# Mixture of experts with soft routing: the third product of the main phase split a second time

## The chip, the cores and the metric

The kernel runs on one core of one Trainium2 chip. The metric is device time in microseconds, the median of several runs. The engines are TensorE (PE in the profile; PEld is its weight load), VectorE (DVE), ScalarE (ACT), GpSimd (POOL) and SyncE (SP). Here POOL and SP mostly issue DMA transfers.

## The reference

Every token takes part in all eight experts, weighted by a softmax of its router logits.

```python
# x: 16 x 512 x 512, router_logits: 16 x 512 x 8, expert_weights: 8 x 512 x 2048, all float32
probs = exp(router_logits - max) / sum
for e in range(8):
    output += probs[:, :, e:e+1] * matmul(x, expert_weights[e])     # 16 x 512 x 2048
```

Written as one product, `output = Z W`. Z has 8192 rows (the tokens) and 8 x 512 columns (x times the probability of each expert), W has 8 x 512 rows and 2048 columns.

## The kernel before

**Two levels of Strassen's products.** The token rows are cut into pieces of 256 (HQ); piece 2q is a, piece 2q+1 is b. With the experts in two halves and the 2048 columns in two halves of 1024, each pair (a, b) is a 2 x 2 block product, done with seven products P1 to P7 in place of eight (Winograd's form). Each of these is itself a product of K = 4 experts x 512 with 1024 columns. Four of the seven (P1, P5, P2, P4) are split once more: the function `sub_product` takes two pieces of 256 rows at once, and does seven inner products in place of eight; `inner_weights` makes the seven weights from four blocks by three or four subtractions. P1, P5 and P2 are kept in DRAM (`kept`, one tensor for each pair), P4 goes to the output as a first part of one quarter.

**The main phase** does the three that are left, P6, P3 and P7, for all q from 0 to 15, one unit of 128 rows of a and 128 rows of b at a time (u = 0, 1), and in it for each half n of 512 columns. For each (q, u, n):

- three loads of kept results, m1, m5 and m2 (`from_kept`, on SP);
- ScalarE copies m1 into a PSUM bank x (L511), and P6's 16 matmuls add to it. The sum is called U2 in the change's title;
- C11 = m1 + m2 on VectorE, and out by POOL (`put`, L506);
- m1 = x + m5 on VectorE (U2 + P5), then P3's 16 matmuls into a bank of their own, and C12 = P3 + m1, out by POOL;
- P7's 16 matmuls into bank x; ScalarE copies it (L522), and POOL adds that to the output in DRAM, over P4 (an accumulating transfer, L523);
- C22 = x + m5 on VectorE, put off to the beginning of the next turn (`late`), out by POOL.

The left operands of the next unit are made on VectorE in seven steps (`operands`), spread over the turn: x times probabilities (z from xT and pT), and subtractions of two z tiles.

**Order.** A scheduler orders instructions and assigns buffers. In the main phase VectorE is kept in the order of the program (`pinned[0] = True` in `dve`); on the other engines the scheduler chooses. Each engine takes its instructions in order, and so do the two queues' issuers, SP and POOL: an instruction that waits holds those behind it. A tile whose buffer is to be used again waits until all that read the earlier tile are done, a transfer from it included.

**Buffers.** `wpool` has 12 tiles of 1 MB (weights), `zpool` 12 (left operands), `xpool` 8, and 21 `h` tiles of 128 x 512 float32 are handed out in turn (`h_tile`). There are eight PSUM banks.

**Lines in the profile.** Helpers issue most instructions: L103 is every tensor_tensor on VectorE (`tt`), L114 every plain transfer on SP (`sp`), L117 weight and x casts on POOL (`pool`), L123 every matmul (`mm`); L342 is `keep` in `sub_product`. So groups are told apart by their tiles.

Of the kernel before, what the change touches and what calls it, by code (L numbers as in the profile page):

```python
# [32 lines left out]
def kernel(  # L33
# [27 lines left out]
    out_f = out.flatten_outer_dims()  # L61

    dram = ctx.enter_context(tc.tile_pool(name="dram", bufs=1, space=bass.MemoryType.DRAM))
    wpool = ctx.enter_context(tc.tile_pool(name="wpool", bufs=12))
    zpool = ctx.enter_context(tc.tile_pool(name="zpool", bufs=12))
    xpool = ctx.enter_context(tc.tile_pool(name="xpool", bufs=8))
    spool = ctx.enter_context(tc.tile_pool(name="spool", bufs=5))
    hpool = ctx.enter_context(tc.tile_pool(name="hpool", bufs=1))
    cpool = ctx.enter_context(tc.tile_pool(name="cpool", bufs=1))

    with tc.tile_pool(name="psum0", bufs=1, space=bass.MemoryType.PSUM) as psum0:
        zero = spool.tile([P, NB], f16, name="zero", tag="xs")
        nc.vector.memset(zero, 0.0)
        every = psum0.tile([P, 8, NB], f32, name="every")
        for i in range(8):
            nc.tensor.matmul(every[:, i, :], zero[:, 0:P], zero, start=True, stop=True)
    psum = ctx.enter_context(tc.tile_pool(name="psum", bufs=8, space=bass.MemoryType.PSUM))

    K8 = 2 * C
    BLOCKS = ((0, 0), (1, 0), (0, 1), (1, 1))

    turn = count()

    def h_tile(shape, dtype):

        return hpool.tile(shape, dtype, name="h", tag=f"h{next(turn) % 21}")

    last = {}  # L90

# [10 lines left out]
    def tt(o, a, b, op):  # L102
        dve(nc.vector.tensor_tensor(out=o, in0=a, in1=b, op=op))  # L103
# [49 lines left out]
    def inner_weights(b, t3=None):  # L153
        t1 = new_w()
        tt(t1, b[0, 1], b[0, 0], SUB)
        yield
        t3 = t3 or b[0, 1]
        tt(t3, b[1, 1], b[0, 1], SUB)
        yield
        t2 = new_w()  # L160
        tt(t2, b[1, 1], t1, SUB)
        t4 = new_w()
        tt(t4, t2, b[1, 0], SUB)
        return {1: b[0, 0], 2: b[1, 0], 3: b[1, 1], 4: t4, 5: t1, 6: t2, 7: t3}


# [13 lines left out]
    P2, P1, PQ = 0, HE, 2 * HE  # L180


    def cast_x(row):
        xs = spool.tile([P, H], f16, name="xs", tag="xs")
        pool(xs, x_f[ds(row, P), :])
        return xs

    NF = 8
    early = [2 * HQ * (j // 2) + P * (j % 2) for j in range(NF)]
    lg0 = []  # L190
    for t in range(2):
        lg0.append(cpool.tile([P, 4, E], f32, name=f"lg0_{t}"))
        for j in range(0, 4, 2):
            sp(lg0[t][:, ds(j, 2)], lg_f[ds(early[4 * t + j], 2 * P), :].rearrange("(j p) e -> p j e", p=P))
    xs0 = [cast_x(row) for row in early[:2]]
    ident = cpool.tile([P, P], f16, name="ident")
    nc.vector.memset(ident, 1.0)
    nc.gpsimd.affine_select(out=ident, in_=ident, compare_op=mybir.AluOpType.is_equal, fill=0.0, base=0,
                            pattern=[[-1, P]], channel_multiplier=1)
    xs0 += [cast_x(row) for row in early[2:4]]  # L200
    b11 = {kn: new_w() for kn in BLOCKS}
    with behind():
        for kn in BLOCKS[:3]:
            for e in range(2):
                cast_w(11, kn, e, b11[kn])
    xs0 += [cast_x(row) for row in early[4:]]
    for e in range(2):
        cast_w(11, BLOCKS[3], e, b11[BLOCKS[3]])

# [51 lines left out]
    def load_x(h):  # L261
        xT = xpool.tile([P, C, HQ], f16, name="xT", tag="x")
        if h in x_dram:
            sp(xT, x_dram[h])
        else:
            for j in range(HQ // P):
                note(nc.sync.dma_start_transpose(out=xT[:, :, ds(j * P, P)], in_=cast_x(h * HQ + j * P)))
            x_new.append((h, xT))
        return xT

# [17 lines left out]

    kept = {r: [dram.tile([2, HQ, NB], f32, name=f"kept{r}_{i}") for i in range(NI)] for r in (1, 2, 5)}

    def half():
        return h_tile([P, NB], f32)

    def out_rows(i, odd, u, cols, n):
        return out_f[ds((2 * i + odd) * HQ + u * P, P), ds(cols * NH + n * NB, NB)]
# [4 lines left out]
        else:  # L300
            sp(kept[r][i][n, ds(u * P, P), :], t)

    def from_kept(r, i, u, n):
        t = half()
        sp(t, kept[r][i][n, ds(u * P, P), :])
        return t

    def sub_product(r, odd, first, w, prep, start=0, zs=None):

        for d in range(start, NI // 2):  # L310
# [19 lines left out]
            for u in range(HQ // P):  # L330
# [7 lines left out]
                    return banks[b]  # L338

                def keep(ps):  # L340
                    t = half()
                    nc.scalar.copy(t, ps)  # L342
                    return t

                def put(t, n, a, b, op):
                    o = half()
                    tt(o, a, b, op)
                    to_kept(r, 2 * d + t, u, n, o)

# [44 lines left out]
    def weights_of_t1():  # L394
        b = {}
        for i, kn in enumerate(BLOCKS):
# [4 lines left out]
        yield  # L401
        ready[5] = yield from inner_weights(b)
    pinned[0] = False
    sub_product(1, 0, P1, w, weights_of_t1(), 1,
                [[z.rearrange("p e c t -> p (e c) t") for z in zz] for zz in z1])

# [13 lines left out]
    def weights_of_t4():  # L420
        b = {}
        for i, kn in enumerate(BLOCKS):
            t, t2 = load(22, kn), load("t1", kn)
            if i < 3:
                b[kn] = load(21, kn)
            yield
            tt(t2, t, t2, SUB)
            store(22, kn, t)
            store("t2", kn, t2)
            if i == 3:  # L430
                b[kn] = load(21, kn)
                yield
            tt(b[kn], b[kn], t2, SUB)
        yield
        ready[4] = yield from inner_weights(b)
    sub_product(2, 0, P2, ready[2], weights_of_t4())


# [1 line left out]

    def weights_of_main():
        for kn in BLOCKS:
            t, t3 = load(22, kn), load(12, kn)
            yield
            tt(t3, t, t3, SUB)
            store("t3", kn, t3)
        yield
        for n in range(2):
            for w, what in ((w6, "t2"), (w3, 22), (w7, "t3")):
                for k in range(2):  # L450
                    w[k, n] = load(what, (k, n), False)
                if n == 0:
                    yield
    sub_product(4, 1, P2, ready[4], weights_of_main())

    def operands(xa, xb, pa, pb, t0):

        z = {}  # L460

        def step(r, x, p, e):
            z[r] = zpool.tile([P, HE, C, P], f16, name="z", tag="z").rearrange("p e c t -> p (e c) t")
            tt(z[r].rearrange("p (e c) t -> p e c t", e=HE),
               x[:, :, ds(t0, P)].unsqueeze(1).to_broadcast([P, HE, C, P]),
               p[:, :, ds(t0, P)].unsqueeze(2).to_broadcast([P, HE, C, P]), MUL)
        return z, [lambda: step(1, xa, pa[0], 0),
                   lambda: step(6, xb, pb[1], 0),
                   lambda: tt(z[6], z[6], z[1], SUB),
                   lambda: step(7, xb, pb[0], 0),  # L470
                   lambda: tt(z[7], z[1], z[7], SUB),
                   lambda: step(3, xa, pa[1], 0),
                   lambda: tt(z[3], z[3], z[6], SUB)]

    def units():
        for q in range(NI):
            xa, p1a = load_x(2 * q), load_p(2 * q, P1)
            xb, pqb = load_x(2 * q + 1), load_p(2 * q + 1, PQ)
            p1b, p2a = load_p(2 * q + 1, P1), load_p(2 * q, P2)
            for u in range(HQ // P):  # L480
                yield q, u, *operands(xa, xb, (p1a, p2a), (p1b, pqb), u * P)

    def prod(z, w, n, ps=None):
        start = ps is None
        if start:
            ps = bank()
        for k in range(2 * K8):
            mm(ps, z[:, k, :], w[k // K8, n][:, k % K8, :], start and k == 0, k == 2 * K8 - 1)
        return ps

    it = units()
    following = next(it)
    for step in following[3]:
        step()
    pinned[0] = True
    late = []
    while following:
        q, u, z, _ = following
        following = next(it, None)
        steps = following[3] if following else []  # L500
        for n in range(2):
            m1, m5, m2 = (from_kept(r, q, u, n) for r in (1, 5, 2))

            def put(odd, cols, o, a, b, op, q=q, u=u, n=n):
                tt(o, a, b, op)
                nc.gpsimd.dma_start(out=out_rows(q, odd, u, cols, n), in_=o)  # L506

            for args in late:
                put(*args)
            x = bank()  # L510
            nc.scalar.copy(x, m1)  # L511
            put(0, 0, m2, m1, m2, ADD)
            for step in steps[4 * n:4 * n + 2]:
                step()
            prod(z[6], w6, n, x)
            tt(m1, x, m5, ADD)
            for step in steps[4 * n + 2:4 * n + 4]:
                step()
            put(0, 1, m1, prod(z[3], w3, n), m1, ADD)
            prod(z[7], w7, n, x)  # L520
            c21 = half()
            nc.scalar.copy(c21, x)  # L522
            nc.gpsimd.dma_start(out=out_rows(q, 1, u, 0, n), in_=c21, accum_op=ADD)  # L523
            late = [(1, 1, m5, x, m5, ADD)]
            late = [(a, b, c, d, e, f, q, u, n) for a, b, c, d, e, f in late]
    for args in late:
        put(*args)

# [1 line left out]
_INS = ['x', 'router_logits', 'expert_weights']  # L530
_OUTS = [((16, 512, 2048), 'float32')]
# [25 lines left out]
```

## Time and profile before

| what | value |
|---|---|
| median of 3 runs | 1479.03 us (1478.55 to 1479.06) |
| the profiled execution's own time | 1482.83 us |
| its span, first to last instruction | 1481.1 us |
| mean granted TensorE clock | 0.992 |
| HBM read, written | 184.84 MB, 163.77 MB |
| matmuls ps<-w,z (L123) | 6672 |

A line of a group gives line, engine, operation, tiles, shapes and count, then total busy time and mean nanoseconds of one; behind the next bar stands the engine's idle time just before these instructions, with what ended most of it. "PE ps L123 <- DVE h L103: 11.8, 7, 3.0" in the view of waits says that matmuls of line 123 waited for VectorE's line 103, for 11.8 us in all, 7 times, at most 3.0. In a windows view each line is a stretch of time with the busy time (and count) of PE, PEld, DVE, ACT and POOL, the granted clock, the DMA engines' busy share, and GB/s. The mean of a matmul (380 ns) is longer than the distance from one to the next, since matmuls are pipelined; the same holds for VectorE and ScalarE by about 0.1 us. Landing is the time from a transfer's issue to its last semaphore update.

### The profile page before, as it was taken

Reading aid. Unit: us, or ns where it says so; the run is one execution under the profiler, and the core shown is the slowest. Engines: PE = TensorE matmul, PEld = TensorE weight load, DVE = VectorE, ACT = ScalarE, POOL = GpSimd, SP = SyncE. Lnnn points to the kernel's source line nnn. Section 1 sums busy time; section 2 is a strip of 40 time slices with the busy share of each in tenths; the row PEclk is TensorE's granted clock in tenths of the full one; section 3 lists DMA queues with packets and bytes.
Section 4 is the critical chain, followed back from the end, with each engine's and each line's share of the span. In section 5 each row is a group of like instructions: output and inputs, shape, how many; then the busy total and the mean of one; then the engine's idle time right before and its main releaser. Section 6 shows DMA issues by size and latency. Waiting matters only on the chain. (4 is left out here: it accounts for less than half of the span.)

```text
span 1481.1 us, 18273 instructions
## 1 busy us (share of the span) xinstructions
PE 1457.9 (98%) x6712; PEld 657.9 (44%) x6712; DVE 956.7 (65%) x1084; ACT 231.5 (16%) x414; POOL 243.4 (16%) x397
## 2 busy tenths in 40 slices
PE   7999999999999999999999999999999999999997
PEld 2444444444444444444444444444444444444443
DVE  4866676656586777766764566665666666565662
ACT  3211121111111121211111001011010101101010
POOL 3111100111000000010101222222222222222221
PEclk8999999999999999999999999999999999999999
DMA  9979967899749994379959887877777777777753
GB/s 174 198 187 259 266 166 182 199 264 255 210 152 305 362 333 148 114 225 258 320 191 319 275 229 212 234 209 219 212 213 210 205 233 207 227 220 214 214 142 91
DMA packets 195801, 327.83 MB, mean 221 GB/s; under 512 B 54784, under 2 KB 84480, under 8 KB 190080
## 3 DMA queue, kind: packets, MB, share of 16 engines
q1 hardware_dynamic: 136192, 203.97, 44.3%
q0 software_dynamic: 59520, 122.71, 35.4%
q8 instruction: 52, 0.85, 0.3%
q14 instruction: 37, 0.30, 0.1%
HBM read 184.84 MB, written 163.77 MB: 235 GB/s over the span
## 5 line engine op out<-in xcount | busy, mean ns | idle before, releaser
L123 PE MATMUL ps<-w,z 128*128 128x512 f16 x6672 | 1444.1, 380 | 3.0 <-DVE h L103 3.0
L123 PEld LDWEIGHTS <-z 128*128 128x128 f16 x6672 | 653.7, 98 | 793.2 <-issue 8.3
L103 DVE TENSOR_TENSOR h<-ps,h 128x512 f32<-128x512 f32 x378 | 260.4, 689 | 416.9 <-ACT h L522 213.2
L103 DVE TENSOR_TENSOR z<-xT,pT 128x2048 f16<-128x2048 f16 x248 | 297.1, 1220 | 19.4 <-PE ps L123 11.1
L103 DVE TENSOR_TENSOR z<-z 128x2048 f16<-128x2048 f16 x220 | 268.0, 1220 | 32.9 <-PE ps L123 24.9
L342 ACT COPY h<-ps 128x512 f32<-128x512 f32 x248 | 145.5, 587 | 601.6 <-PE ps L123 593.2
L506 POOL DMA_DIRECT2D out_dram<-h x192 | 115.3, 640 | 371.1 <-DVE h L103 353.3
L522 ACT COPY h<-ps 128x512 f32<-128x512 f32 x64 | 37.5, 586 | 600.8 <-issue 380.7
L117 POOL DMA_DIRECT2D xs<-in_x_dram x72 | 38.6, 539 | 312.4 <-DMA xT<-xs 304.3
L523 POOL DMA_DIRECT2D out_dram<-h x64 | 56.6, 885 | 177.0 <-ACT h L522 173.1
L103 DVE TENSOR_TENSOR w<-w 128x4096 f16<-128x4096 f16 x32 | 73.0, 2287 | 6.0 <-PE ps L123 3.1
L117 POOL DMA_DIRECT2D w<-in_expert_weights_dram x40 | 30.0, 766 | 131.9 <-DVE w L141 83.7
L103 DVE TENSOR_TENSOR h<-h,ps 128x512 f32<-128x512 f32 x62 | 42.4, 683 | 12.0 <-PE ps L123 12.0
L103 DVE TENSOR_TENSOR h<-h 128x512 f32<-128x512 f32 (+1 forms) x67 | 45.8, 684 | 2.7 <-issue 2.6
L117 POOL DMA_DIRECT2D w<-wd x12 | 6.5, 540 | 204.3 <-DVE w L141 134.9
L511 ACT COPY ps<-h 128x512 f32<-128x512 f32 x64 | 38.1, 596 | 0.0
L231 DVE CAST z<-ps 128x256 f16<-128x256 f32 (+1 forms) x24 | 11.2, 509 | 16.9 <-PE ps L123 16.7
L123 PE MATMUL ps<-h,xs 128*128 128x512 f16 x32 | 11.3, 490 | 8.9 <-DVE h L103 8.9
L117 POOL DMA_DIRECT2D w<-wdt x12 | 6.5, 546 | 32.8 <-DMA wdt<-w 11.9
L229 ACT CAST z<-ps 128x256 f16<-128x256 f32 (+1 forms) x24 | 9.5, 456 | 10.7 <-PE ps L123 10.7
L123 PEld LDWEIGHTS <-xs 128*128 128x128 f16 x32 | 3.2, 110 | 16.4 <-issue 14.9
L385 ACT COPY h<-ps 128x512 f32<-128x512 f32 x8 | 4.7, 586 | 18.3 <-PE ps L123 18.3
(24 smaller groups left out, 19.7 us busy)
## 6 DMA issues: line engine op xcount, KB each, us to landing
out_dram<-h POOLq DMA_DIRECT2D x256, 256.0 KB, 5.0
kept<-h SPq DMA_DIRECT2D x192, 256.0 KB, 4.3
h<-kept SPq DMA_DIRECT2D x192, 256.0 KB, 3.3
pT<-p_dram SPq DMA_DIRECT2D x124, 256.0 KB, 5.0
w<-in_expert_weights_dram POOLq DMA_DIRECT2D x40, 512.0 KB, 12.9
out_dram<-h SPq DMA_DIRECT2D x64, 256.0 KB, 5.4
xT<-x SPq DMA_DIRECT2D x60, 256.0 KB, 4.6
wdt<-w SPq DMA_DIRECT2D x12, 1024.0 KB, 7.8
```

The costliest lines, as they stand in the source:

```text
L103: dve(nc.vector.tensor_tensor(out=o, in0=a, in1=b, op=op))
L117: note(nc.gpsimd.dma_start(out=o, in_=i))
L123: nc.tensor.matmul(ps, z, w, start=start, stop=stop, skip_group_check=True)
L229: note(nc.scalar.copy(o, src_i))
L231: dve(nc.vector.tensor_copy(o, src_i))
L342: nc.scalar.copy(t, ps)
L385: nc.scalar.copy(o, ps[j])
L506: nc.gpsimd.dma_start(out=out_rows(q, odd, u, cols, n), in_=o)
L511: nc.scalar.copy(x, m1)
L522: nc.scalar.copy(c21, x)
L523: nc.gpsimd.dma_start(out=out_rows(q, 1, u, 0, n), in_=c21, accum_op=ADD)
```

## The change

P3 too is now split a second time, for q from 1 on. To have its inner products' two row blocks, the main phase takes a whole pair at once: 256 rows of a with 256 rows of b. A quarter (t, n) is 128 of the 256 rows and 512 of the 1024 columns. For each q:

- P6, all four quarters one after the other, each in a bank seeded with m1; after each, v = x + m5 (U2 + P5) into an `h` tile of class "u";
- on VectorE, `inner()`: four sums of half-size tiles (128 x 8 x 128), written over the z tiles of step `a11`;
- P7, all four quarters, in the same four banks, with C21 and C22 as before;
- P3 as seven inner products of 8 matmuls each, in four more banks x, b, q and d. Products 1, 6 and 7 add up in x, 5 and 3 in q; b is seeded with v00 and d with -v10 by ScalarE (`nc.scalar.mul`). v11 and v01 are added to on VectorE as x and q grow; four puts make C12. The last, `o10`, is put off to the beginning of the next q.
- For q = 0 P3 is plain, on the blocks w3 as they are, while VectorE begins on the inner weights of w3 (`sums`).

The next pair's operands are made by `ahead(...)`, its first two quarters' loads and C11 by `early(j)`, during the present pair. VectorE's program order for q > 0 is: `o10`; `s4(0)`, v of quarter 0; `s4(1)`, v of 1; c11 of 2, `a11(0)` of the next pair, v of 2; c11 of 3, `a11(1)`, v of 3; `inner()`; m5 of 0, `s2(0)`, m5 of 1, `s2(1)`, m5 of 2, m5 of 3; `s3(0)`; put 0; the next pair's c11 of 0; v11; v01; c11 of 1; put 1; put 2; `s3(1)`.

`h` tiles are now 15, shared out by use: in the main phase 5 for "m" (m1, m2 and c21), 4 for "v" (m5), 4 for "u" (v) and 2 for "r" (r1, r3), each class in turn. `wpool` goes from 12 to 15, `zpool` from 12 to 10. In the stages before, `h` tiles are 3 for x casts, 4 for `keep`, and 8 or 11 for results; x is cast 256 rows at a time into one tile; the first eight casts share one weight tile; t3 = T22 - T12 stays on chip as w7 rather than going to DRAM and back; `inner_weights` makes its last subtraction later.

The diff, cut to its core:

```diff
-    wpool = ctx.enter_context(tc.tile_pool(name="wpool", bufs=12))
-    zpool = ctx.enter_context(tc.tile_pool(name="zpool", bufs=12))
+    wpool = ctx.enter_context(tc.tile_pool(name="wpool", bufs=15))
+    zpool = ctx.enter_context(tc.tile_pool(name="zpool", bufs=10))
...
-        return hpool.tile(shape, dtype, name="h", tag=f"h{next(turn) % 21}")
+    def h_tile(shape, dtype, use="any"):
+        mine, i = places[use]
+        places[use][1] = (i + 1) % len(mine)
+        used[mine[i]] = next(turn)
+        return hpool.tile(shape, dtype, name="h", tag=f"h{mine[i]}")
...
+    share(m=5, v=4, u=4, r=2)
+    QUARTERS = ((0, 0), (0, 1), (1, 1), (1, 0))
...
+        def load_kept(self, j):
+            tn = QUARTERS[j]
+            self.m1[tn] = from_kept(1, self.q, *tn, "m")
+            self.m5[tn] = from_kept(5, self.q, *tn, "v")
+
+        def c11(self, j):
+            tn = QUARTERS[j]
+            m2 = from_kept(2, self.q, *tn, "m")
+            tt(m2, self.m1[tn], m2, ADD)
+            self.put(0, 0, tn, m2)
...
+        for j, tn in enumerate(QUARTERS):
+            if j > 1:
+                rows.load_kept(j)
+                rows.c11(j)
+            if j < 2:
+                rows.s4(j)
+            else:
+                ahead("a11", j - 2)
             x = bank()
-            nc.scalar.copy(x, m1)
+            nc.scalar.copy(x, rows.m1[tn])
+            plain(x, 6, w6, tn, False)
+            v = half("u")
+            tt(v, x, rows.m5[tn], ADD)
...
+        if q == 1:
+            inner3 = finish(sums)
+        if q:
+            z3 = rows.inner()
+        for j, tn in enumerate(QUARTERS):
+            x, m5 = xs[j], rows.m5[tn]
+            plain(x, 7, w7, tn, False)
+            c21 = half("m")
             nc.scalar.copy(c21, x)
+            rows.put(1, 0, tn, c21, accum_op=ADD)
+            tt(m5, x, m5, ADD)
+            rows.put(1, 1, tn, m5)
+            if j < 2:
+                ahead("s2", j)
...
+        ahead("s3", 0)
...
+        v00, v01, v11, v10 = vs
+        x = prod(1, "x")
+        r1 = half("r")
+        nc.scalar.copy(r1, x)
+        put(0, prod(2, "b", v00), r1, ADD)
+        early(0)
+        r5 = prod(5, "q")
+        tt(v11, r5, v11, ADD)
+        prod(6, "x")
+        tt(v01, x, v01, ADD)
+        early(1)
+        put(1, prod(3, "q"), v01, ADD)
+        prod(7, "x")
+        r3 = half("r")
+        nc.scalar.copy(r3, x)
+        put(2, x, v11, ADD)
+        ahead("s3", 1)
+        d = prod(4, "d", v10, -1.0)
+
+        def o10(put=put, r3=r3, d=d):
+            put(3, r3, d, SUB)
```

## The prediction

> **What bounds the kernel now.** I read the page first (busy shares and slices), then TensorE's waits, then the main phase in windows, then one cycle of it in the timeline, and last the landing times of the transfers that the change hangs on.
>
> ```profile
> span 1481.1 us, 18273 instructions
> ...
> PE 1457.9 (98%) x6712; PEld 657.9 (44%) x6712; DVE 956.7 (65%) x1084; ACT 231.5 (16%) x414; POOL 243.4 (16%) x397
> ...
> PE   7999999999999999999999999999999999999997
> ...
> DMA  9979967899749994379959887877777777777753
> ```
> TensorE is busy for all of the span but the first and the last slice; VectorE, the next, is at 65%. The waits of TensorE by who ended them:
> ```profile
> PE ps L123 <- DVE h L103: 11.8, 7, 3.0
> ```
> Seven waits, 11.8 us; six of them (8.9 us) are in the opening, one of 3.0 us stands at 841 us, where the main phase begins. From there to 1471 us TensorE waits for nothing. The main phase in three stretches of about two pieces of 256 rows a and 256 rows b ("a pair" from here on, one value of q):
> ```profile
> core 0: us, PE busy (x) PEld busy (x) DVE busy (x) ACT busy (x) POOL busy (x), PEclk, DMA share, GB/s
> 848.00:890.00 42.00, 42.00 (x196) 18.98 (x195) 26.04 (x30) 4.32 (x8) 10.10 (x16) 1.00 0.82 236
> 890.00:931.00 41.00, 41.00 (x191) 18.62 (x190) 26.03 (x30) 4.31 (x8) 10.09 (x16) 1.00 0.76 213
> ```
> TensorE is full at clock 1.00, VectorE has 26 of 41 us, and the DMA engines are already busy 76 to 82%. One quarter of a pair in the timeline (start, duration, engine and instruction):
> ```profile
> 1108.45 0.59 ACT L522 COPY h<-ps 128x512 f32<-128x512 f32 x1 [9.28 <-issue]
> 1108.93 0.60 ACT L511 COPY ps<-h 128x512 f32<-128x512 f32 x1
> 1109.07 0.69 DVE L103 TENSOR_TENSOR h<-ps,h 128x512 f32<-128x512 f32 x1 [3.33 <-ACT h L522]
> ...
> 1109.68 0.68 DVE L103 TENSOR_TENSOR h<-h 128x512 f32<-128x512 f32 x1
> 1110.06 1.26 POOL L506 DMA_DIRECT2D out_dram<-h  x2
> 1110.28 1.22 DVE L103 TENSOR_TENSOR z<-z 128x2048 f16<-128x2048 f16 x1
> 1111.41 1.22 DVE L103 TENSOR_TENSOR z<-xT,pT 128x2048 f16<-128x2048 f16 x1
> ...
> 1118.81 0.59 ACT L522 COPY h<-ps 128x512 f32<-128x512 f32 x1 [9.28 <-issue]
> ```
> From one L522 to the next is 10.36 us for 48 matmuls: 215.8 ns each, 41.44 us a pair. VectorE's instructions start closer than their durations: 0.60 us after a 0.69 us add, 1.13 after a 1.22 us operand step. ScalarE's copies follow at 0.48.
>
> **The gain.** The built program has 6592 matmuls of L123's kind and the opening's instead of 6712 in all: 120 fewer, 8 in each of the 15 pairs from q = 1 on (seven products of 8 in place of 8 times 8). 120 x 215.8 ns = 25.9 us on the path that sets the end. TensorE alone would need 184 x 0.2158 = 39.7 us a pair.
>
> **What is added to VectorE.** Per pair, before, 16 adds and 14 operand steps. After: 18 adds (4 c11, 4 v, 4 m5, 6 around P3), the same 14 steps, now of 2 x 4 x 256, and 4 half-size sums of `inner()`. A half-size sum is in no row; the line through 1220 ns for 2048 and 2287 for 4096 gives 0.69, and 0.72 with the step between dependent ones. A dependent step starts 1.25 after its predecessor (two took 2.47 at 470.76). So 18 x 0.60 = 10.8, six pairs of steps at 1.25 + 1.13 = 14.3, two single ones 2.3, `inner()` 2.8: 30.2 us of 39.7. In sum that is hidden. It is hidden only if VectorE isn't held up.
>
> **What holds it up.** VectorE runs in program order, and one wait closes a ring. In the built order of ScalarE the four seeds of the next pair's x banks stand ahead of the copy `r3`. `put(2)` on VectorE reads the same bank as `r3` and comes after it. The seed of quarter 3 needs its m1 load; with five "m" tiles in turn, that load takes the tile of the next pair's c11 of quarter 0 and waits until that one's put has landed. So from the add `c11(0)` to `put(2)`: VectorE to POOL 0.30 (add ends 1109.76, L506 starts 1110.06); landing of the put; 0.06; landing of the load (SP, L114); 0.06; seed, next copy's start 0.48; `r3` 0.59; 0.03. That is L = 1.52 + put + load. Queued behind `put(2)` are the second `s3` pair, `o10`, both `s4` pairs, the v adds that free the banks for P7, `inner()`, the m5 adds, both `s2` pairs, the first `s3`, `put(0)`, and the following c11(0). That is 14 adds 8.4 + six step pairs 14.3 + two steps 2.3 + `inner()` 2.8 = 27.8 us. The ring turns once a pair: no pair can be shorter than 27.8 + 1.52 + put + load.
>
> No such ring exists before: there a c11 put holds a tile out of 21. The landings of puts on POOL (first line), and of kept loads on SP (second), over 870 to 1400 us, each as least/median/most:
> ```profile
> DMA to landing us min/median/max: 2.6/5.1/7.4
> ```
> ```profile
> DMA to landing us min/median/max: 2.5/3.0/5.8
> ```
> The 2.6 is a put by itself. In groups of three (one accumulating) it is 5.3, and a load among them takes 4.8:
> ```profile
> out_dram<-h POOLq DMA_DIRECT2D x3, 256.0 KB, 5.3
> h<-kept SPq DMA_DIRECT2D x1, 256.0 KB, 4.8
> ```
> That was 1109 to 1112 us. With four loads issued just ahead, at 1146 to 1148 us, a put took the longest:
> ```profile
> pT<-p_dram SPq DMA_DIRECT2D x3, 256.0 KB, 4.8
> h<-kept SPq DMA_DIRECT2D x1, 256.0 KB, 4.6
> out_dram<-h POOLq DMA_DIRECT2D x1, 256.0 KB, 7.4
> ```
> The bounds of a pair: lone transfers 29.3 + 2.6 + 2.5 = 34.4, far under 39.7; the group's values 29.3 + 5.3 + 4.8 = 39.4, just under; the longest of each 29.3 + 7.4 + 5.8 = 42.5, over the 41.4 of before. I take a put of 7.0 and a load of 5.5, 41.8 us: this put is the last of some seven in ten microseconds, two of them accumulating, and in the built order of SP six or more kept loads fall in the same stretch; the row with four loads ahead is nearest. If VectorE is late, its m5 puts, which alternate with the accumulating ones in POOL's order, come in a bunch, which makes the put later still.
>
> Here a rule weighs against the row. The Trainium skill, "DMA: Bandwidth & Descriptors", section "Anatomy of one DMA — SWDGE (gpsimd) path", gives a transfer from POOL 2.0 us plus its bytes over 436 KB per us: an estimate of 2.6 for 256 KB. The lone put agrees. By the rule the pair is 34.5 us, the ring never binds, and the whole 25.9 us come in. But it is the price of one transfer by itself, and the median here is twice that; the trace decides.
>
> So 15 pairs x (41.8 - 41.44) = +5.4 us against the matmul-bound cycle of before, the 25.9 swallowed.
>
> **The rest of the change.** Three weight sums fall into q = 0, which has no `inner()` and no six adds, and one (2.3 us) into q = 1 ahead of `inner()`; I add 2.3 for the pair that starts the ring, between 0 (room of 9 us in VectorE's sum) and 7. The w3 loads now wait for weights that the stage before still uses, and have the 27.5 us of q = 0's P6 and P7; four of 1 MB at the 15 us of `w<-wdt` overlap within it: nothing, some 10 us if they went one by one. The t3 stores and loads (8 MB) go: they were under full slices of TensorE, no gain. ScalarE gets four more copies a pair, 12 x 0.59 = 7.1 us of 41: nothing by its sum; the seeds of b and d are queued ahead of their products. Ten z tiles instead of twelve, twelve h tiles instead of 21 and one 256-row cast in the stages before: seven z tiles live, so the late one of the next round waits for the last product and is used four products of 1.73 us later; 0, at most one such 1.2 us step in each of 31 rounds. The eight first casts in one weight tile and the same opening matmuls: within 1 us both ways. The tail is as it was, one add, put and drain.
>
> **The sum.** 1481.1 + 5.4 + 2.3 = 1488.8 us of span. The profiled span stands 2.1 above the median of the runs, 1479.03; so 1486.7, call it 1487 us.
>
> **Rivals.** The other side: the landings stay at the group's 5.3 and 4.8 or below, the ring fits, and TensorE sets the pair. Whole gain: 1479.0 - 25.9 + 2.3 = 1455. For it: lone values, and on time a pair's accumulating puts are 3.4 us apart. Against: six of ten microseconds of DMA time are taken already by less bunched work. In part: put + load of 11.3 gives 40.6 and 1479.0 - 12.6 + 2.3 = 1469. It decides at put + load = 12.0, where the ring is 41.3 and makes good the 2.3 us. A draw (3 us either way, 0.2 a pair) lies between 11.8 and 12.2. Much slower: the bunching feeds itself, put 9, load 6, pair 44.3: 1479 + 43 + 2 = 1524; nothing in the trace lands that late. That the matmuls don't go away is excluded by the instruction list. That VectorE is the bound by its sum alone is not: 30.2 + a few waits stays under 39.7.
>
> **How the numbers follow.** Ring a little over the old cycle (1482 to 1512): 0.48, the forecast. Much slower: 0.08. Within 0.2% (1476 to 1482), about what a measurement of this kernel can tell: 0.10. Gain in part: 0.24. Whole gain: 0.10. So faster 0.34, same 0.10, slower 0.56. The range 1457 to 1512 leaves out half of the whole gain and the much slower case; the forecast's own is 1482 to 1512.
>
> **What would show it.** Right: TensorE idles before L123's kind released by VectorE's adds, once or twice a pair from q = 1 on; VectorE waits about 14 us after `put(1)`, released by ScalarE's `r3`; c11 puts of quarter 0 land after 6 us or more; about 6592 matmuls. Wrong: a full TensorE row with pairs of 39.7 us, or landings near 3 us; or idle time before P3's first product, which would be `inner()`, not the ring.

## The result, and the profile after

| | before | after |
|---|---|---|
| median | 1478.79 us (1477.96 to 1479.06, 4 runs) | 1451.66 us (1451.36 to 1453.97, 4 runs) |
| profiled execution, its span | 1482.83, 1481.1 us | 1451.38, 1449.7 us |
| matmuls ps<-w,z | 6672 | 6552 |

After over before is 0.982 (95% interval 0.980 to 0.984): faster by 27.1 us by the medians. The forecast was 1487 us, and its range began at 1457. The rival that came true is the whole gain (1455), to which the forecast gave a chance of 0.10.

The page of the changed kernel, the lines that answer to those shown of before:
```profile
span 1449.7 us, 18074 instructions
...
PE 1429.4 (99%) x6592; PEld 645.5 (45%) x6592; DVE 1022.8 (71%) x1178; ACT 272.3 (19%) x482; POOL 230.4 (16%) x361
...
PE   7999999999999999999999999999999999999997
...
DMA  9969986999748995367865877878777777777774
```
TensorE is full in the same 38 slices, with 120 instructions fewer. VectorE has gone from 956.7 to 1022.8 us. In the changed kernel L114 is every tensor_tensor on VectorE, L134 every matmul, L125 plain transfers on SP, L533 the puts on POOL. TensorE's waits for VectorE, from its view of waits:
```profile
PE ps L134 <- DVE h L114: 10.8, 8, 2.5
```
It was 11.8 us in seven waits before. Two of the eight waits are in the main phase (1.1 us at 879 and 0.7 us at 1078 us); no stall once or twice a pair has come. The main phase in stretches, as for the kernel before (us, then busy time and count of PE, PEld, DVE, ACT, POOL, then clock, DMA share, GB/s):
```profile
848.00:890.00 42.00, 40.89 (x191) 18.46 (x189) 32.68 (x36) 8.27 (x15) 10.57 (x17) 1.00 0.80 236
890.00:931.00 41.00, 41.00 (x192) 18.58 (x191) 31.03 (x38) 6.79 (x13) 10.16 (x16) 1.00 0.74 219
930.00:969.70 39.70, 39.70 (x186) 17.99 (x184) 30.52 (x37) 6.75 (x13) 10.12 (x16) 1.00 0.79 229
```
The first holds one stall, in the pair q = 1. The last is one steady pair: 39.70 us, all of it TensorE's, and 30.5 us of VectorE (forecast 39.7 and 30.2). From the first matmul of each pair to that of the next, 12 of the 15 pairs from q = 1 on take 39.71 us and the others 40.98, 40.55 and 39.90. Each of the 15 was 41.44 before.

The landings over 870 to 1400 us, puts on POOL, then kept loads on SP:
```profile
DMA to landing us min/median/max: 2.5/4.9/8.7
```
```profile
DMA to landing us min/median/max: 2.4/4.6/8.1
```
Puts have kept their median (5.1 before) with a longer tail (7.4); kept loads went from 3.0 to 4.6. One turn of the ring that the forecast rested on, from the timeline (start, duration, engine and instruction, then the idle time before and who ended it):
```profile
1117.09 0.68 DVE L114 TENSOR_TENSOR h<-h 128x512 f32<-128x512 f32 x1
1117.46 1.14 POOL L533 DMA_DIRECT2D out_dram<-h  x2 [1.59 <-DVE h L114]
...
1124.19 0.69 DVE L114 TENSOR_TENSOR h<-h 128x512 f32<-128x512 f32 x1 [5.06 <-DMA h<-kept]
1124.80 0.68 DVE L114 TENSOR_TENSOR h<-ps,h 128x512 f32<-128x512 f32 x1
1125.17 1.14 POOL L533 DMA_DIRECT2D out_dram<-h  x2 [6.57 <-DVE h L114]
...
1127.73 0.59 ACT L571 COPY ps<-h 128x512 f32<-128x512 f32 x1 [1.36 <-DMA h<-kept]
1128.26 0.58 ACT L644 COPY h<-ps 128x512 f32<-128x512 f32 x1
1128.87 0.69 DVE L114 TENSOR_TENSOR h<-ps,h 128x512 f32<-128x512 f32 x1 [3.39 <-ACT h L644]
```
The ring is there, step for step. The c11 add of quarter 0 ends at 1117.77. Its put is the second of the two on POOL: issued at 1118.06, landed at 1123.88. The m1 load that wanted its tile goes out at once and lands at 1127.66:
```profile
1123.89 0.32 SPq L125 DMA_DIRECT2D h<-kept  x1
```
Then come the seed (L571), `r3` (L644) and `put(2)` at 1128.87. The `put(2)` before began at 1090.00, so VectorE's part is 1117.77 - 1090.00 = 27.77 us. The forecast was 27.8. But the put took 5.8 and the load 3.8, not 7.0 and 5.5.

The same reading for each turn, as means (the first turn begins it and has no predecessor; the last has no load). "L" is the end of c11(0) to the start of `put(2)`, a turn is from one `put(2)` to the next. The other rows are of experiments below, whose matmuls are the same:

| kernel | VectorE's part, typical | put | load | L | turn | TensorE's 184 matmuls |
|---|---|---|---|---|---|---|
| after | 27.77 | 6.4 | 4.1 | 11.95 | 39.9 | 39.7 |
| one more half-size sum (s1twice) | 28.49 | 6.4 | 3.9 | 11.85 | 40.4 | 39.7 |
| `inner()` twice (inner2) | 30.42 | 6.8 | 4.5 | 12.8 | 43.2 | 39.7 |
| the same, six "m" tiles (inner2_m6) | 30.42 | 7.0 | 4.6 | 12.5 | 42.9 | 39.7 |
| the same, C21 put plainly (inner2_plainc21) | 30.42 | 5.4 | 4.4 | 11.3 | 41.8 | 39.7 |

In the row with six "m" tiles the put and the load are those of c11(0) and its tile as in the other rows, but the path that ends last there is another one (its experiment is below), so they don't add up to L.

In the changed kernel the ring is 27.77 + 11.95 = 39.7 us long, and TensorE's pair is 39.7: the two tie. The mean turn is 39.9: in three of the turns VectorE also waited, by way of ScalarE's copy L587, for TensorE's last P7 product (up to 0.9 us).

### The profile page after: what moved, and what is told of

Same layout as the page of the kernel before. It is cut to its first block, busy times and chain, and to the rows that moved or that the text cites. A ratio compares the mean times of both kernels' runs of the same rounds, so it can differ in the third digit from the quotient of the medians.

```text
span 1449.7 us, 18074 instructions
## 1 busy us (share of the span) xinstructions
PE 1429.4 (99%) x6592; PEld 645.5 (45%) x6592; DVE 1022.8 (71%) x1178; ACT 272.3 (19%) x482; POOL 230.4 (16%) x361
## 4 chain that ended last, share of the span: by engine, by line
PE 52%; issue 34%; POOL 11%; DVE 1%; DMA 1%; POOLq 0%; ACT 0%; SPq 0%; DVEq 0%; ACTq 0%
PE ps L134 52%; POOL out_dram L533 11%; DVE h L114 0%; DVE z L243 0%; POOLq L533 0%; DMA out_dram<-h 0%; DMA h<-kept 0%; DMA lg<-in_router_logits_dram 0%; POOL w L128 0%; DVE z L114 0%; ACT L182 0%; POOLq L676 0%; SPq L125 0%; ACT lg L182 0%; DVE h L184 0%
## 5 line engine op out<-in xcount | busy, mean ns | idle before, releaser
L134 PE MATMUL ps<-w,z 128*128 128x512 f16 x6552 | 1415.9, 379 | 1.8 <-DVE h L114 1.8
L134 PEld LDWEIGHTS <-z 128*128 128x128 f16 x6552 | 641.3, 98 | 776.3 <-issue 4.3
L114 DVE TENSOR_TENSOR h<-ps,h 128x512 f32<-128x512 f32 x389 | 266.1, 687 | 269.2 <-PE ps L134 73.1
L114 DVE TENSOR_TENSOR z<-xT,pT 128x2048 f16<-128x2048 f16 x248 | 299.5, 1219 | 31.6 <-PE ps L134 31.6
L114 DVE TENSOR_TENSOR z<-z 128x2048 f16<-128x2048 f16 x280 | 303.6, 1108 | 7.8 <-DVE z L114 0.5
L356 ACT COPY h<-ps 128x512 f32<-128x512 f32 x248 | 145.6, 587 | 601.4 <-PE ps L134 595.2
L533 POOL DMA_DIRECT2D out_dram<-h x256 | 162.3, 660 | 538.9 <-DVE h L114 500.1
L114 DVE TENSOR_TENSOR h<-h 128x512 f32<-128x512 f32 (+1 forms) x67 | 46.0, 687 | 71.9 <-DMA h<-kept 71.8
L587 ACT COPY h<-ps 128x512 f32<-128x512 f32 x64 | 37.5, 586 | 299.0 <-PE ps L134 204.0
L114 DVE TENSOR_TENSOR w<-w 128x4096 f16<-128x4096 f16 x36 | 82.3, 2287 | 5.6 <-DMA w<-wdt 4.0
L571 ACT COPY ps<-h 128x512 f32<-128x512 f32 x64 | 37.5, 589 | 191.2 <-DMA h<-kept 187.8
L128 POOL DMA_DIRECT2D h<-in_x_dram x32 | 22.5, 704 | 280.4 <-DMA xT<-h 244.7
L114 DVE TENSOR_TENSOR h<-h,ps 128x512 f32<-128x512 f32 x77 | 52.6, 683 | 11.6 <-PE ps L134 10.9
L134 PE MATMUL ps<-h,w 128*128 128x512 f16 x32 | 10.7, 469 | 9.0 <-DVE h L114 9.0
L620 ACT ACTIVATE ps<-h 128x512 f32<-128x512 f32 x30 | 18.2, 608 | 0.0
L633 ACT COPY h<-ps 128x512 f32<-128x512 f32 x15 | 8.8, 587 | 16.4 <-PE ps L134 16.4
L134 PEld LDWEIGHTS <-w 128*128 128x128 f16 x32 | 3.1, 108 | 16.3 <-issue 14.5
L644 ACT COPY h<-ps 128x512 f32<-128x512 f32 x15 | 8.7, 581 | 7.6 <-PE ps L134 7.6
```

The source lines that it names most:

```text
L128: note(nc.gpsimd.dma_start(out=o, in_=i))
L134: nc.tensor.matmul(ps, z, w, start=start, stop=stop, skip_group_check=True)
L533: nc.gpsimd.dma_start(out=out_rows(self.q, odd, tn[0], cols, tn[1]), in_=o, **how)
L571: nc.scalar.copy(x, rows.m1[tn])
L620: nc.scalar.mul(banks[b], seed, scale)
L633: nc.scalar.copy(r1, x)
```

## Experiments

All are edits of the changed kernel. Ratios are to the kernel before, with a 95% interval.

**Without the inner products** (p3plain): P3 stays plain for every q; all else of the change is kept.
```diff
-        if q == 1:
-            inner3 = finish(sums)
-        if q:
-            z3 = rows.inner()
...
-        if q == 0:
+        if True:
...
-                    next(sums)
...
-    o10()
```


> The changed kernel with P3 plain for every q: 120 matmuls come back, inner(), the seeds of b and d and r1, r3 go; the whole-pair order, the pools and the stages before stay. If the gain is the matmuls alone (120 x 215.8 ns = 25.9 us): 1451.7 + 25.9 = 1477.6 us. If the new order and buffers brought part of the gain by themselves, less than 1474; if they cost something that the changed kernel pays too, still 1477.6, and if the plain form suffers in the new order, more than 1481.

Measured: 1476.47 us (1474.98 to 1477.84), 0.998 [0.998, 0.999]. Of the 27.1 us, 24.8 go with the inner products, against 25.9 for the matmuls removed; 2.1 us (against the 1478.6 us of the kernel before, measured beside this run) come with the rest taken together: the order, the new stages, the pools and the start of the main phase.

**Is the ring there?** (inner2): the sums of the left operands are made twice, 2.65 us more on VectorE, same result.
```diff
         if q:
+            rows.inner()
             z3 = rows.inner()
```


> The changed kernel with inner() done twice (the same four sums again, same values): 2.76 us more of VectorE in each pair from q = 1 on, nothing else changed, and VectorE's sum 33 us of 39.7. If the ring from c11 of quarter 0 over its put, the m1 load, the fourth seed, r3 and put 2 back to c11 is what VectorE runs in, and is as long as TensorE's pair: each pair 39.7 + 2.8 = 42.5, 14 pairs, about 1490 us (1480 to 1496). If VectorE is simply hidden by its sum and the ring has room: 1452 us.

Measured: 1496.62 us (1493.01 to 1500.05), 1.011 [1.010, 1.013]. TensorE's waits, and a stretch of 40 us:
```profile
PE ps L134 <- DVE h L114: 44.3, 19, 5.2
```
```profile
930.00:970.00 40.00, 36.50 (x170) 16.33 (x169) 32.25 (x40) 6.14 (x11) 10.12 (x16) 1.00 0.72 199
```
VectorE has 7.8 us idle in these 40 while TensorE waits 3.5 us for it. This isn't VectorE's sum of work; it is something that holds it. The median rose by 45 us, and 15 x 2.65 is 40. From the turns above, 14 x (43.2 - 39.7) = 49, and the span rose by 48.6. TensorE's waits alone don't make up these 48.6 us: in the main phase it stood still for 35.6 us in this execution, against 1.8 in the changed kernel. Most of the rest went in seven stretches, of 3.4 us or once 6.8, at half its granted clock, each beside a stall. One of them:
```profile
1012.50:1015.90 3.40, 3.40 (x9) 1.21 (x8) 0.17 (x1) 0.00 (x0) 0.00 (x0) 0.50 1.04 339
```
The lower clock isn't the cause. From each `put(2)` to the next c11(0), VectorE took 30.41 to 30.42 us in all 13 turns, so it never waited for a product of TensorE there; it waited for `r3`. The ring is real, and the changed kernel has no room in it.

**How little is enough?** (s1twice): only the first of the four half-size sums is done twice, 0.7 us.
```diff
             tt(s1, a21, a22, ADD)
+            tt(s1, a21, a22, ADD)
             tt(s2, s1, a11, SUB)
```


> The changed kernel with the first of inner()'s sums done twice: 0.66 us more of VectorE per pair. If the ring is within 0.1 us of TensorE's pair: 14 x 0.6 = 8 to 9 us more, 1460 us. If the landings of the ring become shorter as it falls behind TensorE (there is a margin of some tenths): 1452 to 1456. If VectorE is hidden by its sum: 1452.

Measured: 1463.14 us (1461.62 to 1466.01), 0.990 [0.988, 0.991], 11.5 us over the changed kernel; 15 x 0.72 = 10.8.
```profile
PE ps L134 <- DVE h L114: 18.1, 17, 2.9
```
Of the seventeen waits six are in the opening and eleven in the main phase, each in a pair of its own: this is near the picture that the forecast drew (once or twice a pair), and 0.7 us of VectorE's work a pair were enough to bring it about. Here the ring runs at its own pace, slower than TensorE's (VectorE's part was 28.48 or 28.49 in all 13 turns), and its put and load still take 6.4 and 3.9. With VectorE's part of the changed kernel that is 27.77 + 1.53 + 10.3 = 39.6. So TensorE's pace doesn't make the ring 39.7 in the changed kernel; as far as these runs show, the two lengths only happen to be alike.

**Is the link a tile?** (inner2_m6): with `inner()` twice, six "m" tiles in place of five, so that the m1 load of quarter 3 doesn't take c11(0)'s tile. (One class "r" tile is given up for it; in the lines below `r3` follows the seed at once, so it isn't that tile which it waits for.)
```diff
-    share(m=5, v=4, u=4, r=2)
+    share(m=6, v=4, u=4, r=1)
```


> inner() twice as in inner2, but with six tiles for m and one for r, so that the m1 load of quarter 3 takes the tile of m1 of quarter 0 and not that of its c11: the ring is cut, VectorE's work is the same as in inner2. If the ring is the cause: 1452 us, within 3. If it is VectorE's amount of work: as inner2, 1480 or more if that is slow.

Measured: 1496.83 us (1493.76 to 1498.41), 1.012 [1.010, 1.013]. The expectation failed: not one microsecond came back. The timeline says why:
```profile
1091.93 2.00 POOL L533 DMA_DIRECT2D out_dram<-h  x3 [1.55 <-DVE h L114]
```
```profile
1100.93 3.23 SPq L125 DMA_DIRECT2D h<-kept  x4
```
```profile
1107.74 0.59 ACT L571 COPY ps<-h 128x512 f32<-128x512 f32 x1 [2.98 <-DMA h<-kept]
1108.26 0.58 ACT L645 COPY h<-ps 128x512 f32<-128x512 f32 x1
1108.88 0.69 DVE L114 TENSOR_TENSOR h<-ps,h 128x512 f32<-128x512 f32 x1 [9.79 <-ACT h L645]
```
(L645 is `r3` here.) The third of the three puts, the m5 of quarter 3, was issued at 1093.05 and landed at 1101.84. In the four loads on SP the next m5 load of quarter 3 stands ahead of the m1 load. It waits for this put's landing and goes out at 1101.90. The m1 load, which needs no such tile now, stands behind it in the queue: out at 1102.32, landed at 1107.66. There are two paths of much the same length from VectorE's adds to the fourth seed: one by a tile, one by SP's order. The forecast saw only the first. In the changed kernel too the second is close behind: that m5 load went out at 1122.29, 1.6 us ahead of the m1 load.

**Cut both at their common end** (inner2_r3v): both paths enter VectorE by ScalarE's order, where `r3` stands behind the fourth seed. With `inner()` twice, VectorE makes `r3` itself, in program order, just ahead of `put(2)`.
```diff
-        nc.scalar.copy(r3, x)
+        dve(nc.vector.tensor_copy(r3, x))
```


> inner() twice as in inner2, and r3 copied by VectorE instead of ScalarE, so that put 2 and o10 no longer stand behind ScalarE's seeds of the next pair: VectorE has 0.6 us more work than in inner2 (33.6 us by its sum). If the ring through ScalarE's order is what made inner2 slow: 1451 to 1455 us. If it is VectorE's amount of work or waits of its own: 1497 or more.

Measured: 1454.94 us (1451.35 to 1456.85), 0.984 [0.982, 0.985]: 41.7 of inner2's 45 us are gone, though VectorE has still more to do.
```profile
PE ps L134 <- DVE h L114: 12.2, 7, 3.7
```
```profile
930.00:970.00 40.00, 40.00 (x187) 18.16 (x186) 34.69 (x43) 5.77 (x11) 10.44 (x17) 1.00 0.77 230
```
VectorE at 34.7 of 40 us holds nobody up, where at 32.3 it cost 3.5 us a stretch. The link by ScalarE's order is what closes the ring. The 3.3 us that stay belong to the pair q = 1, which took 45.23 us (40.98 in the changed kernel); all later ones took 39.71.

**The same without the doubling** (r3v): only the diff above.

> The changed kernel with r3 copied by VectorE and nothing else. The ring is gone; TensorE had about 2 us of idle time left in the main phase: 1449 to 1452 us. If VectorE's 0.6 us more per pair count as they did in s1twice: 1463.

Measured: 1451.32 us (1449.68 to 1452.43), 0.981 [0.980, 0.983], level with the changed kernel. So the ring costs the changed kernel next to nothing: at its length of 39.7 it only ties. The two longer pairs behind q = 1 are gone (all take 39.71 from q = 2 on):
```profile
PE ps L134 <- DVE h L114: 9.6, 7, 2.4
```

**The first pair too** (allsplit_r3v): with r3v, P3 of q = 0 is split as well; its branch goes, and the weight sums are made after the P7 products of q = 0.
```diff
-        if q == 1:
-            inner3 = finish(sums)
-        if q:
-            z3 = rows.inner()
+        z3 = rows.inner()
...
+        if q == 0:
+            inner3 = finish(sums)
```


> As r3v, with q = 0 split a second time too: the four weight sums are made after the m5 adds of q = 0, and 8 matmuls fewer: 1.7 us under r3v if the w3 loads and the sums are in time, 1448 to 1450 us; up to 8 us over it if P3 of q = 0 waits for the sums.

Measured: 1449.26 us (1448.80 to 1449.76), 0.980 [0.979, 0.982], the fastest here, 2.4 us under the changed kernel.
```profile
PE 1428.8 (99%) x6584; PEld 645.0 (45%) x6584; DVE 1046.1 (72%) x1204; ACT 261.6 (18%) x462; POOL 228.4 (16%) x361
```
Eight matmuls fewer are 1.7 us of it.

**What do the accumulating puts cost the ring?** (inner2_plainc21): with `inner()` twice, where the ring sets the time and so measures itself, C21 is put plainly. P4's part of that quarter of the output is lost by it.
```diff
-            rows.put(1, 0, tn, c21, accum_op=ADD)
+            rows.put(1, 0, tn, c21)
```


> inner() twice, with C21 written by plain puts instead of accumulating ones (P4's part is left out of that quarter of the output). If the ring's put lands late because accumulating puts stand ahead of it: its landing falls from about 6.4 us to 4 and the pair by as much, 14 x 2.4 = 34 us under inner2's 1497, 1463. If the landing doesn't depend on them: 1497.

Measured: 1478.82 us (1476.8 to 1479.9), 17.8 us under inner2, or 1.2 us a pair. About half of what I had put on it. In the table above c11(0)'s put went from 6.8 to 5.4 and the load stayed. The median of all puts from 870 to 1400 us, of inner2 and then of this kernel:
```profile
out_dram<-h POOLq DMA_DIRECT2D x198, 256.0 KB, 4.7
```
```profile
out_dram<-h POOLq DMA_DIRECT2D x202, 256.0 KB, 4.0
```
So the company of accumulating puts is a part of why a put takes 6.4 and not 2.6, but not the whole.

## Why the prediction was wrong, step by step

- **The gain**, 120 x 215.8 ns = 25.9 us: right. 12 of 15 pairs take the 39.7 us that TensorE needs alone, and undoing the inner products cost 24.8.
- **VectorE's sum**, 30.2 us a pair: right (30.5 measured), and so was that a sum doesn't matter much: the same engine was hidden at 34.7 and in the way at 32.3.
- **The ring and VectorE's part in it**, 27.8 us and 1.52 of fixed steps: right (27.77; 11.95 - 6.4 - 4.1 = 1.5).
- **The failed step** is "I take a put of 7.0 and a load of 5.5, 41.8 us". They measured 6.4 and 4.1, together 10.4 in place of 12.5; the deciding 12.0 lies between. The mechanism stood, and two terms of its sum were too large. The ring became 39.7 and not 41.8, and a ring that only ties with TensorE costs nothing. Of the 2.1 us too much, 1.4 are the load's.
- **Why the landings were shorter** is known in part. The row that I took them from had four loads issued just ahead; I expected six or more in the same stretch, and that lateness feeds itself. The kept loads did come in that stretch, but not as a bunch: seven of the nine go out within 0.1 us of the landing of some put. Between 1113.5 and 1124.9 us SP sends them one by one, 0.4 to 2.5 us apart. While VectorE waits, POOL has nothing to put (from 1118.6 to 1125.2 us it issues none), so the m1 load flies when the puts ahead of it have landed. The loads of that stretch, in order of issue from 1115.98 on, took 6.1, 5.7, 5.1, 4.2, 4.1, 4.3, 3.8 (the m1 load) and 3.8. Where the m1 load goes out with such puts still on their way, as in inner2_m6, it took 5.6 us on average (4.8 to 6.6), the forecast's 5.5. This fits, but no run isolates it, so why the landings were shorter stays open. That lateness eases itself is not the answer: in inner2, where VectorE is later, they were longer (6.8 and 4.5) than in the changed kernel.
- **The rule that was weighed** gave 2.6 us for a put, and through it the whole gain, which came; but that is luck, since its put isn't the one measured (6.4). The group's row (5.3 + 4.8 = 10.1) was the nearest of the bounds, and it gave 39.4, just under TensorE's 39.7. (Where I weighed the rivals I took the DMA engines as busy in six of ten microseconds; the windows that I had shown say 0.76 to 0.82.)
- **The rest of the change**: 2.3 us for starting the ring were 1.3 in the pair q = 1, where VectorE makes the inner operands for the first time; with `inner()` twice that pair took 4.3 us more (45.23 in inner2_r3v against 40.98). The rest I put at nothing, and taken together it was a small gain: 2.1 us by the medians, as the run without the inner products shows.

The profiled spans differ by more, 31.4 us: 25.9 for matmuls, 1.3 for an opening that is done earlier (what follows its last matmuls begins at 52.5, before 53.8), 4.6 for the first pair of the main phase, 1.9 for the tail, less 2.3 for the three longer pairs. The 4.6 are a stall of 3.0 us and a stretch of reduced clock in the profiled execution of before. (I had put this stall at the beginning of the main phase; that begins at 803 us, and the stall is near the end of its first pair.)
```profile
840.00:843.50 3.50, 1.33 (x7) 0.49 (x5) 3.50 (x5) 0.00 (x0) 2.54 (x4) 1.00 1.05 403
843.50:847.50 4.00, 3.21 (x9) 1.14 (x9) 2.47 (x4) 0.00 (x0) 0.55 (x1) 0.57 1.06 335
```
That execution was 4.0 us longer than its kernel's median, so this part belongs at least partly to it alone.

Of the signs that I named, the matmul count and a c11(0) put of 6 us or more (mean 6.4) came. VectorE was held by `r3`, but for 3.9 us a pair and not for 14:
```profile
DVE h L114 <- ACT h L644: 58.9, 15, 6.6
```
The rest of L went into the adds in between and into waiting for the load of c11(1): 62.6 us in 14 waits, 4.5 each. TensorE's idle time once or twice a pair did not come. I took it that a held VectorE means a held TensorE. But VectorE runs behind TensorE here (`r3` begins about 5 to 8 us after its product is done), and as long as a turn isn't longer than TensorE's pair, it stays as far behind and no more.

## What to carry to other kernels

Where an engine waits in program order for a copy that stands in another engine's queue, write down the ring (own work, fixed steps, landings) and compare it with the bound engine's pair: all above it is paid in every turn, all below costs nothing, and where the spread of the landings reaches to both sides of it, as here (39.4 to 42.5, where 39.7 is the whole gain and 41.3 none), both outcomes need a chance to match; I gave 0.10 to the one that came. Look for every path that ends in the late instruction before freeing one: a tile more did nothing, since SP's order gave a second path, while changing who makes `r3`, the last common step, removed both. Whether a change that came out well has room is found by adding a small known work to the suspected ring: 0.7 us showed that there was none.

## What the runs showed of the hardware

- Plain puts were slower in the company of accumulating ones: with them a plain 256 KB put in the ring took 6.8 us, without them 5.4 (inner2 and inner2_plainc21), while the load that follows was the same (4.5 and 4.4).
- A kept load in company took from 3.4 to 5.7 us in the same place of the changed kernel's pairs, and the put 5.7 to 7.2. With transfers at three quarters of the DMA engines' share, one landing can't be told to better than a microsecond or two from rows of another arrangement.
- In the profiled execution of inner2, seven of the nine stalls of TensorE of 2.5 us and more in the main phase stood beside a stretch of 3.4 us (once 6.8) at a granted clock of 0.50; the five shorter ones did not.
